# Constants of a hybrid encoder kernel packed so that the tiles TensorE reads begin at multiples of 512 bytes

## The chip, the core and the metric

The kernel runs on one core of a Trainium2 chip. The metric is the device time of one execution in microseconds (us); lower is better. Before the change the median of three runs is 2232.35 us (2230.22 to 2233.93).

The core's memory for operands, SBUF, has 128 partitions; a tile of shape 128 x 512 in float32 takes 2048 bytes in every partition. A tile's address is its byte offset within a partition. This text speaks of addresses by what is left of them after division by 512, and calls that the tile's **offset**.

## What is computed

The reference is a two-layer encoder on 512 tokens of width 1024, in float32. Cut to what matters here:

```python
for i in range(2):
    x = x + 0.5 * swiglu_ffn(rmsnorm(x, ffn1_norm[i]), ffn1_w1[i], ffn1_w2[i])
    h = rmsnorm(x, mix_norm[i])
    x = x + (s5_gla_mixer(h, ...) if i == 0 else retention_mixer(h, ...))
    x = x + 0.5 * swiglu_ffn(rmsnorm(x, ffn2_norm[i]), ffn2_w1[i], ffn2_w2[i])
return rmsnorm(x, final_norm)

def swiglu_ffn(h, w1, w2):              # w1: 1024 x 5632, w2: 2816 x 1024
    gate, up = jnp.split(h @ w1, 2, axis=-1)
    return (silu(gate) * up) @ w2
```

`s5_gla_mixer` holds a diagonal state-space model (S5) beside a gated linear attention, `retention_mixer` a retention layer; both are mostly projections by weight matrices as well.

## The kernel before, in words

**Arithmetic.** TensorE multiplies in `float32r`, which keeps fewer bits than float32. So each operand is split in two float32r tiles, a high part (`yh`, `wh`, `ph`, `qh`, `g`, `rh`, `vh`, `oh`, `ch`) and what is left (`yl`, `wl`, `pl`, `ql`, ...), and `mm3` (lines 193 to 195) makes three matmuls in place of one: high by high, high by low, low by high. In `T.matmul(ps, a, b)` the tile `a` is the *stationary* operand (a block of 128 x 128 that is loaded into the array first, the row LDWEIGHTS of the profile) and `b` the *moving* one (256 or 512 columns that stream through it). The profile names a matmul `mm<-b,a`: `mm<-y,wh` has `y` moving and `wh` stationary.

**Order of work.** The first FFN (`ffn`) uses plain products, with 512 moving columns. The three others (`ffn7`) cut each product of w1 into seven half-size products (Strassen's scheme): 256 moving columns, stationary blocks from `wh`/`wl` (raw weights, two of the seven), from `ph`/`pl` (sums of weights, four of the seven) and from `qh`/`ql` (one of the seven). Their second product by w2 again has 512 columns. The S5 part (line 843 and lines 885 to 887 among others) multiplies in full float32. Weights come by DMA from the SP queue, in order, into four buffers `raw` (line 177), ScalarE (ACT) and VectorE (DVE) split them, and for most of them a DMA from the GpSimd (POOL) queue adds `raw` into the low part (`lows`, line 189).

**Where tiles lie.** Pools are laid out one behind the other. The first pool, `const`, holds `x` (16384 bytes), then the small constants; behind it lie the pools `weights` (raw, wh, wl), `temps`, `operands` (the 28 tiles `y`), and behind these the pool of the stage that runs (`g`, `ph`, `pl`, `qh`, `ql`, `rh`, `vh`, ...). Almost every tile in these later pools is a multiple of 1024 bytes, so their offsets are all set by how many bytes the constants take, and by one small tile `rt` (128 x 2, two buffers of 32 bytes) in `temps`:

```python
gains = cp.tile([128, 7 * 8 + 4 + 16 + 4], F32, name="gains")          # 320 bytes
ident = cp.tile([128, 128], F32, name="ident")                         # 512
less = cp.tile([128, len(SEVEN) * 4], F32, name="less")                # 48, takes 64
rho8 = cp.tile([128, NG], F32, name="rho8")                            # 128
ones = cp.tile([128, 128], F32, name="ones")                           # 512
eps = cp.tile([128, 1], F32, name="eps")                               # 4, takes 32
```

`rho8` (decay rates of the S5 scan) is made early in the first FFN on ACT, and read by DVE in the mixer. `less` is used in `operand7`, `rt` in `finish`, the last norm at the end of the kernel.

Of the kernel before, what the change touches and what calls it, by code (L numbers as in the profile page):

```python
# [16 lines left out]
F32 = mybir.dt.float32  # L17
# [16 lines left out]
NG = 32  # L34
TWO_PI = 2.0 * math.pi
SEVEN = (2, 3, 5)
# [14 lines left out]
def encoder(tc, I, out, dbg=None):  # L51
    nc = tc.nc
    V, A, G, T = nc.vector, nc.scalar, nc.gpsimd, nc.tensor
    dma = nc.sync.dma_start
    f32 = lambda ap: ap.bitcast(F32)

    with ExitStack() as ctx:
        cp = ctx.enter_context(tc.tile_pool(name="const", bufs=1))
# [4 lines left out]
        dp = ctx.enter_context(tc.tile_pool(name="scratch", bufs=1, space=DRAM))  # L63
# [4 lines left out]
        yp = ctx.enter_context(tc.tile_pool(name="operands", bufs=28))  # L68
        ytile = lambda dt=F32R: yp.tile([128, S], dt, name="y", tag="y")
        yh, yl = [None] * KT, [None] * KT  # L70
        gains = cp.tile([128, 7 * 8 + 4 + 16 + 4], F32, name="gains")
        ident = cp.tile([128, 128], F32, name="ident")
        less = cp.tile([128, len(SEVEN) * 4], F32, name="less")
        minus = {(n, i): less[:, a * 4 + i:a * 4 + i + 1] for a, n in enumerate(SEVEN) for i in range(4)}
        rho8 = cp.tile([128, NG], F32, name="rho8")
        ones = cp.tile([128, 128], F32, name="ones")
        eps = cp.tile([128, 1], F32, name="eps")
        V.memset(ones, 1.0)
        V.memset(eps, EPS)
        norm_gain = lambda n, i: gains[:, n * 8 + i:n * 8 + i + 1]  # L80
# [7 lines left out]
        rd = dp.tile([4, 128, 2, 512], F32, name="rd")  # L88
        td = dp.tile([NG, 16, 15, 16], F32, name="td")
        ud = dp.tile([512, S], F32, name="ud")  # L90

        def tmp(tag, shape=(128, S), dt=F32):
            return tp.tile(list(shape), dt, name=tag, tag=tag)

        def bank(name="mm"):
            return pp.tile([128, S], F32, name=name, tag="mm")
# [173 lines left out]
        def ffn7(w1, w2, acc, nxt, gp, finish=None):  # L270
# [136 lines left out]
            for q, (ks0, ks1) in enumerate(CHUNKS):  # L407
# [85 lines left out]
                if finish is not None and not more:  # L493

                    steps = []
                    ws = [weights(w2q[n], True) for n in (KT - 2, KT - 1)]
                    for c in (left, right):
                        for n, w in zip((KT - 2, KT - 1), ws):
                            ps = bank()
                            for k in range(ks0, ks1):  # L500
                                second(n, ps, w, [k], ks1, c)
                                if steps and k % 2:
                                    next(steps[0], None)
                            residual(n, ps, c)
                            if n == KT - 2:
                                sq = tmp("tb", (128, H2))
                                A.activation(sq, x[n][:, c], AF.Square)
                                G.tensor_tensor(acc[:, c], acc[:, c], sq, op=ALU.add)
                        steps.append(finish(acc, c))
                    for _ in steps[1]:  # L510
                        pass
# [3 lines left out]
        def s5_prepare(wk):  # L515
# [25 lines left out]
            A.activation(cs, t1, AF.Sin)  # L541
            tt(t2, lr, dt, op=ALU.mult)
            A.activation(mag, t2, AF.Exp)
            A.activation(rho8, t2, AF.Exp, scale=float(TC))
            pr = wk.tile([128, TC + 1, NG], F32, name="pr")
            pi = wk.tile([128, TC + 1, NG], F32, name="pi")
            V.memset(pr[:, 0], 1.0)
# [169 lines left out]
            for st in range(NG // 4):  # L717
                finish(st, *built)
                if st < 7:
                    built = build(st + 1)  # L720
                if st == 2:
                    tabs = rotations()
                elif 3 <= st:
                    if st < 7:
                        rotate_table(st - 3, tabs)
                yield


        def s5_gla(acc, nxt, mp):
# [25 lines left out]
                to_chunks(j, project(W[j])[0])  # L755


            wgk = mp.tile([32, 512], F32, name="wgk")
            dma(wgk, I["wgk"])
            rmask = mp.tile([128, S], F32, name="rmask")  # L760
# [461 lines left out]
        with tc.tile_pool(name="g0a", bufs=14) as ga:  # L1222
            wk_pool = tc.tile_pool(name="s5work", bufs=1)
            wk = wk_pool.__enter__()
            wa = [wk.tile([128, 4, TC + 1, 16], F32, name=f"wa{i}") for i in range(2)]
            pieces = s5_prepare(wk)
            gb = []

            def filler(j):
                if j == 1:  # L1230
                    dma(ident, I["ident"])
                next(pieces, None)
                if j == 12:
                    for _ in pieces:
                        raise RuntimeError("S5 pieces left")
                    wk_pool.__exit__(None, None, None)
                    gb.append(ctx2.enter_context(tc.tile_pool(name="g0b", bufs=18)))

            with ExitStack() as ctx2:
                pick = lambda i: ytile() if i < 12 else (ga if i < 26 else gb[0]).tile([128, S], F32R, name="g", tag="g")  # L1240
                acc = ffn(I["ffn1_w1"][0], I["ffn1_w2"], acc, 1, pick, filler, first)
        show("ffn0")
        with tc.tile_pool(name="mix0", bufs=1) as mp:
            phase[0] = 1
            acc = s5_gla(acc, 2, mp)
            phase[0] = 0
# [14 lines left out]
        def finish(acc, c):  # L1261
            n, blocks = KT - 1, range(c.start // 128, c.stop // 128)
            last = tmp("tb", (128, S // 2))
            A.activation(last, x[n][:, c], AF.Square)
            st = sp.tile([128, S], F32, name="st", tag="st")
            rt = tmp("rt", (128, 2))
            yield
            for i, b in enumerate(blocks):
                T.matmul(st[:, i:i + 1], acc[:, b * 128:(b + 1) * 128], ones[:, 0:1], start=True, stop=False)
                T.matmul(st[:, i:i + 1], last[:, i * 128:(i + 1) * 128], ones[:, 0:1], start=False, stop=True)  # L1270
            A.activation(rt, st[:, 0:2], AF.Sqrt, bias=eps, scale=1.0 / D)
            V.reciprocal(rt, rt)
            diag = tmp("ta", (128, 256))
            for i in range(2):
                V.tensor_scalar_mul(diag[:, i * 128:(i + 1) * 128], ident, rt[:, i:i + 1])
            yield
            yield
            row = bank()
            T.matmul(row[:, 0:256], ones, diag, start=True, stop=True)
            if c.start == 0:  # L1280
                for i in range(n - 1):
                    A.activation(x[i], x[i], AF.Copy, scale=norm_gain(6, i))
            for i in (n - 1, n):
                A.activation(x[i][:, c], x[i][:, c], AF.Copy, scale=norm_gain(6, i))
            yield
            to = out.rearrange("(i p) t -> p i t", p=128)
            for t in (slice(0, 3), slice(3, 6), slice(6, 8)):
                V.tensor_tensor(xs[:, t, c], xs[:, t, c],
                                row[:, 0:256].unsqueeze(1).to_broadcast([128, t.stop - t.start, 256]), op=ALU.mult)
                dma(to[:, t, c], xs[:, t, c])  # L1290

        with tc.tile_pool(name="step3", bufs=1) as gp:
            ffn7(I["ffn2_w1"][1], w2(2), acc, None, gp, finish)
# [109 lines left out]
```

## Time and profile before

| | before |
|---|---|
| median of the runs | 2232.35 us |
| the profiled execution: its time / its span | 2233.29 us / 2231.5 us |
| granted TensorE clock, mean | 0.973 of 2.4 GHz |
| busy share of the span: PE, PEld | 95%, 83% |
| busy share of the span: DVE, ACT, POOL | 60%, 52%, 16% |
| matmuls | 12088 |

The span is the time from the first to the last instruction; the execution's own time has 1.8 us more around it. PE is TensorE's matmul side, PEld its weight loads. Matmuls are pipelined, so the busy time of one (its "mean ns") is longer than the step from one matmul's start to the next one's; the step is what a stream of matmuls costs, and it is read from a timeline as the difference of two starts over the number of matmuls between them.

### The profile page before, as it was taken

Reading aid. Unit: us, or ns where it says so; the run is one execution under the profiler, and the core shown is the slowest. Engines: PE = TensorE matmul, PEld = TensorE weight load, DVE = VectorE, ACT = ScalarE, POOL = GpSimd, SP = SyncE. Lnnn points to the kernel's source line nnn. Section 1 sums busy time; section 2 is a strip of 40 time slices with the busy share of each in tenths; the row PEclk is TensorE's granted clock in tenths of the full one; section 3 lists DMA queues with packets and bytes.
Section 4 is the critical chain, followed back from the end, with each engine's and each line's share of the span. In section 5 each row is a group of like instructions: output and inputs, shape, how many; then the busy total and the mean of one; then the engine's idle time right before and its main releaser. Section 6 shows DMA issues by size and latency. Waiting matters only on the chain.

```text
span 2231.5 us, 31247 instructions
## 1 busy us (share of the span) xinstructions
PE 2121.6 (95%) x12088; PEld 1844.2 (83%) x12088; DVE 1348.5 (60%) x2101; ACT 1169.2 (52%) x1696; POOL 363.8 (16%) x396
## 2 busy tenths in 40 slices
PE   8998999999998989999998999999999998999998
PEld 6877888777878889987988888778888887898897
DVE  7696210178748667568766566545444469766564
ACT  7444444462676454546655354455454557455453
POOL 3431112211021010103111010211111112010101
PEclk9999999998998999999999999999999999999999
DMA  8878888867565564554565464667676756564551
GB/s 233 212 196 220 196 191 189 229 171 210 133 151 143 151 148 139 144 145 123 141 158 154 125 145 120 165 163 176 152 180 151 172 138 159 141 156 137 148 155 48
DMA packets 125076, 357.50 MB, mean 160 GB/s; under 512 B 19808, under 2 KB 34528, under 8 KB 124800
## 3 DMA queue, kind: packets, MB, share of 16 engines
q0 software_dynamic: 41328, 133.19, 33.1%
q1 hardware_dynamic: 83600, 222.33, 29.7%
q8 instruction: 95, 1.56, 0.3%
q14 instruction: 53, 0.43, 0.1%
HBM read 208.17 MB, written 14.12 MB: 100 GB/s over the span
## 4 chain that ended last, share of the span: by engine, by line
PE 62%; DMA 12%; DVE 7%; issue 5%; ACT 5%; POOL 0%; SPq 0%; ACTq 0%; DVEq 0%; POOLq 0%
PE mm L193 20%; PE mm L194 20%; PE mm L195 20%; DMA raw<-in_ffn_w_dram 5%; DMA ql<-raw 4%; DMA wl<-raw 1%; ACT wl L188 1%; DVE pl L221 1%; ACT qh L324 1%; ACT ql L188 1%; ACT sv L336 0%; DMA raw<-in_w2a_dram 0%; DVE y L134 0%; PE st L1142 0%; DMA raw<-in_ab_in_dram 0%
## 5 line engine op out<-in xcount | busy, mean ns | idle before, releaser
L193 PE MATMUL mm<-y,wh 128*128 128x512 f32 (+1 forms) x1304 | 458.9, 352 | 7.9 <-ACT wh L1214 5.0
L195 PE MATMUL mm<-y,wl 128*128 128x512 f32 (+1 forms) x1304 | 454.9, 349 | 5.7 <-DMA wl<-raw 5.7
L194 PE MATMUL mm<-y,wh 128*128 128x512 f32 (+1 forms) x1304 | 456.1, 350 | 0.3 <-DVE y L103 0.3
L180 ACT CAST wh<-raw 128x1024 fp32r<-128x1024 f32 (+1 forms) x227 | 232.0, 1026 | 421.2 <-issue 190.4
L189 POOL DMA_DIRECT2D wl<-raw x221 | 190.7, 864 | 1290.1 <-ACT wl L188 1146.0
L193 PE MATMUL mm<-y,ph 128*128 128x256 f32 x1056 | 312.0, 296 | 59.2 <-ACT sv L336 41.0
L194 PE MATMUL mm<-y,ph 128*128 128x256 f32 x1056 | 308.6, 292 | 1.8 <-DVE y L134 1.8
L195 PE MATMUL mm<-y,pl 128*128 128x256 f32 x1056 | 307.9, 292 | 1.8 <-DVE pl L221 1.8
L193 PEld LDWEIGHTS mm<-y,wh 128*128 128x128 f32 x1304 | 249.2, 191 | 47.1 <-ACT wh L1214 5.4
L195 PEld LDWEIGHTS mm<-y,wl 128*128 128x128 f32 x1304 | 248.3, 190 | 41.0 <-DMA wl<-raw 7.7
L194 PEld LDWEIGHTS mm<-y,wh 128*128 128x128 f32 x1304 | 248.7, 191 | 35.0 <-DVE y L103 2.1
L193 PEld LDWEIGHTS mm<-y,ph 128*128 128x128 f32 x1056 | 211.7, 201 | 65.4 <-ACT sv L336 46.1
L193 PE MATMUL mm<-g,wh 128*128 128x512 f32 (+1 forms) x672 | 259.1, 387 | 0.6 <-ACT g L220 0.6
L194 PE MATMUL mm<-g,wh 128*128 128x512 f32 (+1 forms) x672 | 259.3, 387 | 0.0
L195 PE MATMUL mm<-g,wl 128*128 128x512 f32 (+1 forms) x672 | 258.8, 386 | 0.0
L188 ACT ACTIVATE wl<-raw 128x1024 fp32r<-128x1024 f32 x221 | 233.0, 1055 | 38.4 <-PE mm L194 23.4
L194 PEld LDWEIGHTS mm<-y,ph 128*128 128x128 f32 x1056 | 212.3, 201 | 2.7 <-DVE y L134 2.3
L195 PEld LDWEIGHTS mm<-y,pl 128*128 128x128 f32 x1056 | 211.9, 201 | 2.3 <-DVE pl L221 2.3
L221 DVE TENSOR_TENSOR pl<-sums,ph 128x1024 fp32r<-128x1024 f32 x132 | 160.7, 1222 | 77.2 <-ACT ph L220 76.7
L220 ACT CAST ph<-sums 128x1024 fp32r<-128x1024 f32 x132 | 137.4, 1050 | 68.1 <-PE mm L194 51.2
L193 PEld LDWEIGHTS mm<-g,wh 128*128 128x128 f32 x672 | 126.0, 188 | 27.1 <-ACT g L220 1.7
L195 PEld LDWEIGHTS mm<-g,wl 128*128 128x128 f32 x672 | 126.2, 188 | 26.1
(358 smaller groups left out, 3633.8 us busy)
## 6 DMA issues: line engine op xcount, KB each, us to landing
wl<-raw POOLq DMA_DIRECT2D x221, 512.0 KB, 5.5
raw<-in_ffn_w_dram SPq DMA_DIRECT2D x196, 512.0 KB, 4.0
raw<-in_w2b_dram SPq DMA_DIRECT2D x48, 512.0 KB, 3.3
raw<-in_ret_in_dram SPq DMA_DIRECT2D x48, 512.0 KB, 3.7
ql<-raw POOLq DMA_DIRECT2D x66, 256.0 KB, 4.5
raw<-in_w2a_dram SPq DMA_DIRECT2D x24, 384.0 KB, 3.7
raw<-in_ret_out_dram SPq DMA_DIRECT2D x16, 512.0 KB, 3.6
raw<-in_ab_in_dram SPq DMA_DIRECT2D x13, 512.0 KB, 4.9
```

What stands on the lines that cost most here:

```text
L180: A.copy(h[:, c], raw[:, c])
L188: A.activation(l, raw, AF.Copy, scale=-1.0)
L189: G.dma_start(l, raw, accum_op=ALU.add)
L193: T.matmul(ps, lh, rh, start=first, stop=False, skip_group_check=go_on)
L194: T.matmul(ps, lh, rl, start=False, stop=False, skip_group_check=go_on)
L195: T.matmul(ps, ll, rh, start=False, stop=last, skip_group_check=go_on)
L220: A.copy(hi, src)
L221: V.tensor_tensor(lo, src, f32(hi), op=ALU.subtract)
L324: A.copy(h, raws[j][1][:, hi4])
```

## The change

The small constants are put in one tile `columns` of 384 bytes (gains, less, eps as slices of it), and `rho8` no longer lives in `const`: ACT writes it to a tile of the S5 work pool, a DMA stores it in DRAM (`rhod`), and a second DMA loads it into a tile of the mixer's pool. `rt` becomes a slice of `less`.

```diff
-        gains = cp.tile([128, 7 * 8 + 4 + 16 + 4], F32, name="gains")
+        columns = cp.tile([128, 96], F32, name="columns")
+        gains, less, eps = columns[:, 0:80], columns[:, 80:92], columns[:, 92:93]
         ident = cp.tile([128, 128], F32, name="ident")
-        less = cp.tile([128, len(SEVEN) * 4], F32, name="less")
...
-        rho8 = cp.tile([128, NG], F32, name="rho8")
         ones = cp.tile([128, 128], F32, name="ones")
-        eps = cp.tile([128, 1], F32, name="eps")
...
+        rhod = dp.tile([128, NG], F32, name="rhod")
...
+            rho8 = wk.tile([128, NG], F32, name="rho8")
             A.activation(rho8, t2, AF.Exp, scale=float(TC))
+            dma(rhod, rho8)
...
+            rho8 = mp.tile([128, NG], F32, name="rho8")
+            dma(rho8, rhod)
             wgk = mp.tile([32, 512], F32, name="wgk")
...
-            rt = tmp("rt", (128, 2))
+            rt = less[:, c.start // 128:c.start // 128 + 2]
```

The offsets that the two built programs give their tiles:

| tiles | offset before | after |
|---|---|---|
| raw, wh, wl, and the temporaries (ta, tb, tc, rs, sumsq) | 160 | 0 |
| y, g, ph, pl, qh, ql, rh, rl, vh, vl, oh, ol, ch, cl, sums, sv | 224 | 0 |
| ident | 448 | 0 |
| ones | 128 | 0 |
| vm, wm, w1 of the S5 part | 96 | 0 |
| x (not read by TensorE) | 128 | 128 |

Blocks within these tiles begin at multiples of 512 bytes from the tile's start, so a block has its tile's offset. Before, 160, 224 and 96 are all 32 bytes past a multiple of 64.

The rows of PE, ACT, DVE and POOL stand in the same order in both programs, but for names and for two neighbours on ACT. The SP queue, which issues the loads, gets two more DMAs, and the load of `ident` moves ahead of one load of weights (the third of them, at the start of the kernel). The first place is early in the first FFN; `raw` are weights, `rho_350` is the program's name for the new tile `rho8`, and the brackets name the semaphores a row waits for. Before:

```order
L632 DMA dsk<-in_s5d_dram 16x64 [waits DMAHW3_49]
L177 DMA raw<-in_ffn_w_dram 128x1024 [waits DMAHW4_49,DMAHW5_49,DMASW0_49,Activation_49]
L177 DMA raw<-in_ffn_w_dram 128x1024 [waits DMAHW6_49,DMASW1_49,Activation_49]
L177 DMA raw<-in_ffn_w_dram 128x1024 [waits DMAHW7_49,DMASW2_49,Activation_49]
L177 DMA raw<-in_ffn_w_dram 128x1024 [waits DMAHW2_49,DMASW3_49,Activation_49]
```

And after:

```order
L634 DMA dsk<-in_s5d_dram 16x64 [waits DMAHW3_49]
L177 DMA raw<-in_ffn_w_dram 128x1024 [waits DMAHW4_49,DMAHW5_49,DMASW0_49,Activation_49]
L177 DMA raw<-in_ffn_w_dram 128x1024 [waits DMAHW6_49,DMASW1_49,Activation_49]
L546 DMA rhod<-rho_350 128x32 [waits Activation_49]
L177 DMA raw<-in_ffn_w_dram 128x1024 [waits DMAHW7_49,DMAHW0_49,DMASW2_49]
L177 DMA raw<-in_ffn_w_dram 128x1024 [waits DMAHW2_49,DMASW3_49,Activation_49]
```

The store of `rho8` stands between two loads of weights and waits for ACT. The second place is the start of the mixer's loads, near the end of the first FFN. After (before, the row L761 is missing, and nothing else differs but line numbers):

```order
L177 DMA raw<-in_ab_in_dram 128x1024 x6
L761 DMA rho_3471<-rhod 128x32
L763 DMA wgk<-in_wgk_dram 32x512
L767 DMA rmask<-in_rmask_dram 128x512
L768 DMA cmask<-in_cmask_dram 128x64
L771 DMA tb<-in_gmf_dram 128x512
L771 DMA tb<-in_gmb_dram 128x512
L177 DMA raw<-in_ab_in_dram 128x1024
```

The load of `rho8` is put ahead of the five loads of masks and gate weights.

## Rows read from the trace of the kernel before

**Rows 1.** The page, part 4: chain that ended last, shares of the span by engine.

```profile
PE 62%; DMA 12%; DVE 7%; issue 5%; ACT 5%; POOL 0%; SPq 0%; ACTq 0%; DVEq 0%; POOLq 0%
```

**Rows 2.** Groups by line and shape: count, busy us, mean ns, idle before.

```profile
L193 PE MATMUL mm<-y,ph 128*128 128x256 f32 x1056 | 312.0, 296 | 59.2 <-ACT sv L336 41.0 <-ACT ph L220 16.3 <-ACT y L132 1.9
L193 PE MATMUL mm<-y,wh 128*128 128x512 f32 x776 | 310.0, 400 | 7.9 <-ACT wh L1214 5.0 <-ACT y L102 2.4 <-ACT wh L180 0.3
...
L193 PE MATMUL mm<-g,wh 128*128 128x512 f32 x640 | 250.0, 392 | 0.6 <-ACT g L220 0.6
...
L193 PE MATMUL mm<-y,wh 128*128 128x256 f32 x528 | 148.9, 282 | 0.0
...
L193 PE MATMUL mm<-y,qh 128*128 128x256 f32 x264 | 74.8, 283 | 0.0
...
L193 PE MATMUL mm<-wh,y 128*128 128x512 f32 x160 | 63.8, 401 | 0.4 <-DVE tb L1070 0.4
...
L193 PE MATMUL mm<-oh,wh 128*128 128x512 f32 x128 | 49.7, 388 | 0.0
...
L193 PE MATMUL mm<-ph,vh 128*128 128x512 f32 x64 | 24.9, 393 | 0.0
```

**Rows 3.** Timeline of PE, 2002.9 to 2006 us: start, length, engine, line, instruction.

```profile
2002.62 0.28 PE L193 MATMUL mm<-y,qh 128*128 128x256 f32 x1
...
2004.06 0.28 PE L193 MATMUL mm<-y,wh 128*128 128x256 f32 x1
...
2005.42 0.28 PE L193 MATMUL mm<-y,ph 128*128 128x256 f32 x1
```

**Rows 4.** Timeline of PE, 1243 to 1248 us, first and last of 24.

```profile
1242.66 0.39 PE L194 MATMUL mm<-g,wh 128*128 128x512 f32 x1
...
1247.93 0.39 PE L193 MATMUL mm<-g,wh 128*128 128x512 f32 x1
```

**Rows 5.** Timeline of PE, 1478.4 to 1485 us, first and last of 24.

```profile
1478.45 0.39 PE L193 MATMUL mm<-ph,vh 128*128 128x512 f32 x1
...
1483.66 0.39 PE L195 MATMUL mm<-ph,vl 128*128 128x512 f32 x1
```

**Rows 6.** Timeline of PE, 1455 to 1460 us, first and last of 12.

```profile
1454.73 0.40 PE L194 MATMUL mm<-wl,y 128*128 128x512 f32 x1
...
1457.30 0.39 PE L193 MATMUL mm<-wh,y 128*128 128x512 f32 x1
```

**Rows 7.** Timeline of PE, 425.1 to 428.4 us, first and last of 8.

```profile
425.37 0.63 PE L193 MATMUL mm<-y,wh 128*128 128x512 f32 x1
...
428.36 0.44 PE L194 MATMUL mm<-y,wh 128*128 128x512 f32 x1
```

**Rows 8.** Windows: busy by engine, granted clock (0.50), DMA share, GB/s.

```profile
425.10:428.40 3.30, 3.30 (x10) 2.53 (x9) 0.00 (x0) 0.00 (x0) 0.00 (x0) 0.50 0.99 199
```

**Rows 9.** Timeline of PE in the S5 part, float32 matmuls (two records each).

```profile
544.74 3.40 PE L843 MATMUL mm<-U,vm 128*128 128x64 f32 x29
...
551.40 0.38 PE L885 MATMUL mm<-w,U 128*64 128x128 f32 x2
...
553.14 0.38 PE L887 MATMUL mm<-wm,xi 128*64 128x128 f32 x2
```

**Rows 10.** Timelines of SP, ACT and DVE at the places of rho8.

```profile
30.62 5.49 SPq L177 DMA_DIRECT2D raw<-in_ffn_w_dram  x2
...
30.90 0.21 ACT L544 ACTIVATE rho<-small 128x32 f32<-128x32 f32 x1
...
423.92 1.03 SPq L759 DMA_DIRECT2D wgk<-in_wgk_dram  x1
...
499.43 0.68 DVE L833 TENSOR_TENSOR tc<-rho,cmask 128x512 f32<-128x512 f32 x1
```

**Rows 11.** Groups by line and shape: two DVE instructions.

```profile
L390 DVE TENSOR_TENSOR x<-x,ta 128x512 f32<-128x512 f32 x70 | 47.5, 687 | 1.1
...
L379 DVE TENSOR_TENSOR ta<-ta,rs 128x512 f32<-128x512 f32 x66 | 45.4, 687 | 0.8
```

## The prediction, made before the changed kernel was run

> **What bounds the kernel now.** First I read the chain of work that ended last, because only what lies on it can shorten the span: TensorE (PE) holds 62% of the 2231.5 us, DMA 12%, DVE 7%, ACT 5% [rows 1]. So the step from one matmul to the next is the largest price in this kernel. Second I read how many matmuls of each kind there are [rows 2]. Each row there is one of three lines (193 to 195) of equal count, so a count is taken three times: 4632 matmuls with 512 columns whose stationary block is in `wh`/`wl` (3 x (776 + 640 + 128)), 480 with the weights moving and `y` stationary (3 x 160), 192 with `vh`/`vl` (3 x 64); 3960 with 256 columns and `ph` or `qh` stationary (3 x (1056 + 264)), 1584 with 256 columns and `wh` (3 x 528).
>
> Third I read the step of each kind from timelines, in stretches without a wait, and set the offsets of both operands beside it:
>
> - 256 columns, `y` (offset 224) with `qh` (224): 12 matmuls in 1.44 us, 120.0 ns each; directly behind them the same `y` with `wh` (160): 12 in 1.36 us, 113.3 ns [rows 3].
> - 512 columns, `g` (224) with `wh` (160): 23 in 5.27 us, 229 ns [rows 4].
> - 512 columns, `ph` (224) with `vh` (224): 23 in 5.21 us, 226.5 ns [rows 5].
> - 512 columns, `wh` (160) moving with `y` (224): 11 in 2.57 us, 233.6 ns [rows 6].
>
> At 2.4 GHz one column per clock would be 106.7 and 213.3 ns. Times 2.4, the five steps are 288, 272, about 550, 544 and 560 clocks: 16 to 48 clocks too many. Two things stand in these rows. The surplus depends on where the operands lie: in rows 3 the moving tile, the shape, the neighbours and the engines are the same, and only the stationary tile changes, from offset 224 to 160, and with it 6.7 ns. And it is a matter of supply, not of the array: where the granted clock is 0.50 (1.2 GHz) [rows 8] the same 512 columns take 427 ns (7 in 2.99 us) [rows 7], which is 512 clocks of 1.2 GHz with no surplus. Full float32, which spends two clocks on a column, shows hardly any either: 128 columns take 108.8 ns (16 records in 1.74 us from L885 to L887), 256 clocks and 5 more [rows 9], though all its tiles too lie 32 bytes past a multiple of 64.
>
> **The change, part by part.** PE's program stays as it is, row for row; what moves is every operand, from 224 or 160 to 0.
>
> *Matmuls.* No matmul before has both operands at a multiple of 64 bytes, so the new step has no row and is bounded from both sides. My reading of the surplus: 16 float32r columns are 64 bytes, and a stream that begins 32 bytes past a multiple of 64 touches one piece of 64 bytes more than it holds: 17 for 16 (272 clocks), 33 for 32 (528). What then remains of the rows with equal offsets (288, 544) is 16 clocks in both, a collision of the two streams. After the change all operands have equal offsets and no extra piece: 288 - 16 = 272 clocks, 113.3 ns, for 256 columns, and 544 - 16 = 528, 220.0 ns, for 512. In sum:
>
> - 4632 x (229 - 220.0) = 41.7 us
> - 192 x (226.5 - 220.0) = 1.2 us
> - 480 x (233.6 - 220.0) = 6.5 us
> - 3960 x (120.0 - 113.3) = 26.5 us
> - 1584 x (113.3 - 113.3) = 0
>
> Together 75.9 us. (Some 400 matmuls of smaller groups, `ch`, `rh` and the last halves of `g`, are left out; they would add about 2 us.) The best end for this price is a step with only float32's 5 clocks more than its columns: 517, 215.4 ns, for 512. For 256 columns the loading of the stationary block sets a floor: the row of L843, where 64 columns hardly hide it, has 28 steps in 3.40 - 0.27 = 3.13 us, 111.8 ns for a block of 128 [rows 9]. These give 4632 x 13.6 + 192 x 11.1 + 480 x 18.2 + 3960 x 8.2 + 1584 x 1.5 = 63.0 + 2.1 + 8.7 + 32.5 + 2.4 = 108.7 us. The worst end is the dearest row of each length: 233.6 and 120.0 ns, 33.3 us more than now (4632 x 4.6 + 192 x 7.1 + 1584 x 6.7). I take the middle price, since it is the only one that explains 272, 288 and 544 by whole pieces; about 550 and 560 need one collision more, which I can't derive.
>
> *How much of it reaches the end.* The mean clock is 0.973, so 5.4% of the span is at 1.2 GHz, where nothing is gained: at most 0.946 x 75.9 = 71.8 us. As lower bound I take PE's part of the chain alone: the matmuls counted above fill 4632 x 0.229 + 192 x 0.2265 + 480 x 0.2336 + 3960 x 0.12 + 1584 x 0.1133 = 1871 us, 75.9 is 4.1% of that, and 4.1% of 62% of the span is 56 us; the rest would be given back as longer waits for DMA, ACT and DVE. The middle is 64 us, 84% of the sum.
>
> *The store of rho8* stands on SP between two loads of weights. ACT makes it from 30.90 to 31.11 us; SP issued a load at 30.62 and the next at about 35.8 (the row holds two issues and ends at 36.11) [rows 10]. So the store falls in a free interval of some 4 us: nothing. If ACT were 5 us later there, loads of weights would wait behind it.
>
> *The load of rho8* stands ahead of `wgk` at 423.92 us, whose issue took 1.03 us [rows 10], so what is behind it on SP is up to 1 us late; DVE reads rho8 at 499.43 us, 75 us later. 0 to 1 us; I take 0, because the load of weights behind the masks fills a buffer ahead of its use. The load of `ident`, ahead of the third load of weights, is 64 KB and also nothing.
>
> *Other engines.* `x` already lies at a multiple of 64 before, the temporaries do not; a DVE instruction that writes `x` and one that stays in temporaries have the same 687 ns [rows 11]. So DVE and, by the same measure, ACT gain nothing.
>
> *DMA.* No row tells two offsets of one transfer apart. On the chain DMA has 12% [rows 1], 268 us. I take 0. The Trainium skill, "DMA: Bandwidth & Descriptors", section "How a descriptor splits into AXI transactions", says that a descriptor that does not start on a multiple of 256 bytes pays for the bytes before it; by that, a row of `raw` (4096 bytes at offset 160) would fall from 133 beats of 32 bytes to 128, an estimated 3.8%, or up to 10 us of the chain's DMA. No run here shows it yet.
>
> The sum against the profiled execution's 2233.3 us (0.9 us above the median): 2233.3 - 64 = 2169 us.
>
> **The rivals.**
>
> *The full price goes* (the best end above): 0.84 x 108.7 = 92 us, 2142 us; if no wait gives any back, 0.946 x 108.7 = 103 us, 2130. For it speaks that float32 shows 5 clocks at any offset; against it that equal offsets still cost 288 where 160 against 224 cost 272, so a collision is there that alignment need not remove.
>
> *Only the relation of the two operands counts.* Then all pairs get the price of the equal pairs, 120.0 and 226.5 ns: -4632 x 2.5 - 480 x 7.1 + 1584 x 6.7 = -4.4 us, 2229.6 us. For it speaks that each kind's step is fixed by a pair of offsets; against it nothing in the rows, since the equal pair at 224 is also 32 past a multiple of 64.
>
> *Nothing changes.* The steps would be set by something that goes along with the tile and not with its offset, such as its place in memory. Then 2233 us. Against it: `y` and `oh`, far apart, show the same kind of step with `wh`. The Trainium skill, "SBUF — State Buffer", section "Specifications (TRN2)", speaks for this rival: it gives SBUF lines of 16 bytes, and every tile before begins at a multiple of 32 already, so by it there is nothing to straddle. Rows 3 differ from that page, in that 64 bytes of offset change the step.
>
> *Slower: both streams begin at the same place.* With all offsets 0, the moving and the stationary stream start on the same piece every time, and the collision grows to that of the dearest rows. If only the 256-column matmuls with `wh` go to 120.0 ns, it is 1584 x 6.7 = 10.6 us, 2243 us; at the worst end 0.946 x 33.3 = 31.5 us, 2265 us. It decides as soon as the 512-column step is above 229 ns. For it: the equal pair is the dearer one at 256 columns. Against it: at 512 it is the cheapest.
>
> **How the numbers follow.** The middle price 0.43, the full price 0.17, the relation alone 0.13, nothing 0.09, slower 0.18. About 0.2%, 4.5 us, is what a measurement here can tell from no change. Faster by more than that: the first two and a small part of the third, 0.62; the rest of the third and the fourth, 0.20; slower 0.18. The point is that of the likeliest, 2169 us; its own range is 2155 to 2185. The range for 8 in 10 has to take in the full price and the cases near no change: 2125 to 2245; about 0.05 lies below (a gain of DMA on top), 0.12 above.
>
> **What would show it.** Timelines of PE after: 256-column steps at 113.3 ns for `ph` and `qh` as for `wh`, and 512-column ones at 220.0 ns in all three kinds; at 1.2 GHz still 427 ns. 120.0 and 226.5 would show the relation alone, 111.8 and 215.4 the full price. Beside it idle time of PE that ends on DMA or ACT should grow by some 8 to 20 us. The prediction is wrong if the steps stay or grow, or if they shrink as said and the span doesn't, since the chain then goes over to the loads.

## The result and the profile after

The change made the kernel faster by half a per cent, a fifth of what was forecast: 2219.02 us (median of 12 runs, 2212.49 to 2229.49) against 2231.24 us (12 runs), ratio 0.9948 with a 95% interval of 0.9933 to 0.9963, so about 12 us and not 64. Three further comparisons of the same two kernels gave 0.9935, 0.9953 and 0.9951. The profiled execution below is the slowest of the 12 (2229.49 us, span 2227.7), so steps are read from it and no gain.

The chain that ended last, of the changed kernel, answers to [rows 1]: PE's share fell by 3 points and "issue", time in which nothing that the profile shows was waited for, rose by 3. It says less than it seems to: in three further executions of the same kernel PE holds 59%, 50% and 62%, so shares of one chain don't carry an effect of 0.5%.

```profile
PE 59%; DMA 13%; issue 8%; DVE 7%; ACT 5%; POOL 1%; SPq 0%; ACTq 0%; DVEq 0%; POOLq 0%
```

Timelines of PE in the changed kernel (start, length, engine, line, instruction), in the order of [rows 3], [rows 4], [rows 5] and [rows 6]; last, at the lower clock, [rows 7], with its window as [rows 8].

```profile
1998.09 0.28 PE L193 MATMUL mm<-y,qh 128*128 128x256 f32 x1
...
1999.53 0.28 PE L193 MATMUL mm<-y,wh 128*128 128x256 f32 x1
...
2000.97 0.28 PE L193 MATMUL mm<-y,ph 128*128 128x256 f32 x1
```

```profile
1243.73 0.39 PE L194 MATMUL mm<-g,wh 128*128 128x512 f32 x1
...
1247.36 0.39 PE L195 MATMUL mm<-g,wl 128*128 128x512 f32 x1
```

```profile
1476.69 0.39 PE L193 MATMUL mm<-ph,vh 128*128 128x512 f32 x1
...
1481.91 0.39 PE L195 MATMUL mm<-ph,vl 128*128 128x512 f32 x1
```

```profile
1443.70 0.39 PE L193 MATMUL mm<-wh,y 128*128 128x512 f32 x1
...
1449.14 0.39 PE L193 MATMUL mm<-wh,y 128*128 128x512 f32 x1
```

```profile
441.96 0.63 PE L193 MATMUL mm<-y,wh 128*128 128x512 f32 x1
...
445.38 0.63 PE L195 MATMUL mm<-y,wl 128*128 128x512 f32 x1
```

```profile
441.90:445.80 3.90, 3.90 (x10) 2.97 (x9) 0.00 (x0) 0.00 (x0) 0.00 (x0) 0.50 1.05 281
```

Both 256-column streams of 12 matmuls now take 1.44 us, 120.0 ns a step: `wh` lost the 6.7 ns that it had over `qh`. All 512-column steps are alike: 16 in 3.63 us (226.9), 23 in 5.22 (227.0), 24 in 5.44 (226.7). At granted clock 0.50 it is 427 ns (8 in 3.42 us), as before. These are the steps of the rival "only the relation of the two operands counts", 120.0 and 226.5, in every kind.

Groups of the changed kernel by line and shape (count, busy us, mean ns, idle before): PE's wait for ACT's copies to `sv` is 39.2 us, in [rows 2] 41.0.

```profile
L193 PE MATMUL mm<-y,ph 128*128 128x256 f32 x1056 | 309.8, 294 | 57.6 <-ACT sv L336 39.2 <-ACT ph L220 16.4 <-ACT y L132 1.9
L193 PE MATMUL mm<-y,wh 128*128 128x256 f32 x528 | 152.4, 289 | 0.0
```

### The profile page after: what moved, and what is told of

The parts are those of the page before. It is cut to its first block, busy times and chain, and to the rows that moved or that the text cites. A ratio compares the mean times of both kernels' runs of the same rounds, so it can differ in the third digit from the quotient of the medians.

```text
span 2227.7 us, 31250 instructions
## 1 busy us (share of the span) xinstructions
PE 2115.4 (95%) x12088; PEld 1851.1 (83%) x12088; DVE 1348.3 (61%) x2101; ACT 1169.9 (53%) x1696; POOL 363.4 (16%) x396
## 4 chain that ended last, share of the span: by engine, by line
PE 59%; DMA 13%; issue 8%; DVE 7%; ACT 5%; POOL 1%; SPq 0%; ACTq 0%; DVEq 0%; POOLq 0%
PE mm L193 19%; PE mm L194 19%; PE mm L195 19%; DMA raw<-in_ffn_w_dram 6%; DMA ql<-raw 4%; DMA wl<-raw 2%; ACT wl L188 1%; ACT qh L324 1%; ACT ql L188 1%; DVE pl L221 1%; POOL wl L189 0%; ACT sv L336 0%; DVE y L134 0%; PE st L1146 0%; DVE wl L182 0%
## 5 line engine op out<-in xcount | busy, mean ns | idle before, releaser
L193 PE MATMUL mm<-y,ph 128*128 128x256 f32 x1056 | 309.8, 294 | 57.6 <-ACT sv L336 39.2
L193 PEld LDWEIGHTS mm<-y,wh 128*128 128x128 f32 x1304 | 251.8, 193 | 44.8 <-ACT wh L1218 5.0
L194 PEld LDWEIGHTS mm<-y,wh 128*128 128x128 f32 x1304 | 252.3, 193 | 33.5 <-issue 1.4
L297 ACT CAST wh<-raw 128x1024 fp32r<-128x1024 f32 x66 | 69.3, 1050 | 149.3 <-DMA raw<-in_ffn_w_dram 99.1
```

The costliest lines, as they stand in the source:

```text
L193: T.matmul(ps, lh, rh, start=first, stop=False, skip_group_check=go_on)
L194: T.matmul(ps, lh, rl, start=False, stop=False, skip_group_check=go_on)
L297: A.copy(h, up)
```

## The experiments

Three theories about the step of a matmul stood against each other. **Pieces** (the prediction's): each stream that begins 32 bytes past a multiple of 64 pays. **Relation**: only the difference of the two operands' offsets counts. **The tile**: something that goes with the tile and not with its offset. What else made the 12 us, the DMAs' offsets or the moved constants, was asked beside it. Each experiment is the changed kernel with pads, tiles that nothing uses, unless said otherwise. "Before" is timed anew on the chip of each group.

**1. Offsets by themselves.** This kernel computes no encoder, only streams of matmuls and DMAs:

```diff
+for cols in (512, 256):
+    for r in range(0, 512, 32):
+        group(f"d{r}at0c{cols}x", cols, r, 0)
...
+            T.matmul(ps[:, 0:cols], sta[:, s:s + 128], mov[:, m:m + cols], start=n == 0, stop=n == count - 1)
...
+            G.dma_start(cut(lows[at], at), cut(raws[at], at), accum_op=ALU.add)
```

> This kernel leaves out the whole encoder: it runs 25 float32r matmuls in a row for each pair of offsets (stationary r bytes past the moving one, r from 0 to 480 in steps of 32, and a few pairs at other absolute offsets), with 512 and with 256 columns, and then six loads and six adding DMAs of 512 KB for each of seven offsets. Theory 'relation': the step depends on the difference of the two offsets alone; difference 0 gives 226.7 ns at 512 and 120.0 at 256 at any absolute offset (0, 32, 224), difference -64 gives about 229 and 113.3, +64 about 233 at 512. Rival 'pieces of 64 bytes' (the prediction's): a pair at absolute offset 0 or 64 is some 6.7 ns cheaper than the same difference at 32 or 224. For the adding DMAs, theory 'the DMA's own offset': packets of 4096 bytes at 32, 160 and 224 take about 3% longer (338 against 328 ns in the kernels) than at 0, 128 and 256; rival: no difference by offset, the kernels' 10 ns come from what ran beside them.

Timeline of PE in this kernel; `d192at0` means that the stationary block lies 192 bytes past the moving one, which lies at 0, and `dm64` that it lies 64 below.

```profile
62.66 5.84 PE L72 MATMUL d0at0c512x<-mov,sta 128*128 128x512 f32 x25
68.33 5.99 PE L72 MATMUL d32at0c512x<-mov,sta 128*128 128x512 f32 x25
74.16 6.00 PE L72 MATMUL d64at0c512x<-mov,sta 128*128 128x512 f32 x25
80.00 6.00 PE L72 MATMUL d96at0c512x<-mov,sta 128*128 128x512 f32 x25
...
97.48 5.90 PE L72 MATMUL d192at0c512x<-mov,sta 128*128 128x512 f32 x25
103.22 5.99 PE L72 MATMUL d224at0c512x<-mov,sta 128*128 128x512 f32 x25
109.05 5.84 PE L72 MATMUL d256at0c512x<-mov,sta 128*128 128x512 f32 x25
114.72 5.99 PE L72 MATMUL d288at0c512x<-mov,sta 128*128 128x512 f32 x25
...
155.44 5.83 PE L72 MATMUL d0at32c512x<-mov,sta 128*128 128x512 f32 x25
161.11 5.85 PE L72 MATMUL d0at224c512x<-mov,sta 128*128 128x512 f32 x25
166.79 6.00 PE L72 MATMUL d64at32c512x<-mov,sta 128*128 128x512 f32 x25
172.63 6.00 PE L72 MATMUL d64at64c512x<-mov,sta 128*128 128x512 f32 x25
178.47 5.98 PE L72 MATMUL d64at224c512x<-mov,sta 128*128 128x512 f32 x25
184.29 5.89 PE L72 MATMUL dm64at224c512x<-mov,sta 128*128 128x512 f32 x25
190.01 5.84 PE L72 MATMUL d16at0c512x<-mov,sta 128*128 128x512 f32 x25
195.69 6.00 PE L72 MATMUL d48at0c512x<-mov,sta 128*128 128x512 f32 x25
```

From start to start over 25: difference 0 gives 5.67 us, 226.8 ns, at offsets 0, 32 (5.67) and 224 (5.68) alike; 64 gives 5.84, 233.6, at 0, at 32 and at 64, and 5.82 at 224; 192 gives 5.74, 229.6, and -64 gives 5.72, 228.8; and 256 is like 0 (5.67). Where a stream of 512 columns begins costs nothing; the difference decides, counted modulo 256. "Pieces" falls here, and "the tile" too, since the same two tiles are read in every row.

With 256 columns the picture is less clean. Difference 0 takes 118.8 to 120.4 ns at 0, 32 and 224, and -64 takes 113.6, as the theory says. But a difference of 64 takes 118.0 ns at offset 0 and 117.6 at 64, and 114.4 at 32 and 114.0 at 224. That is not the absolute offset, because a difference of 320 at offset 0, the same modulo 256, takes 114.4 as well. Group 4 comes back to it.

**2. Relation and absolute offset crossed in the whole kernel.** `undo` restores the old offsets (160 and 224) and keeps the rest of the change, `eq224` puts all operands at 224, `rel64` makes the old difference of 64 out of multiples of 64 (weights at 0, `y` and stages at 64).

```diff
+        cp.tile([128, 40], F32, name="pad")                        # undo; eq224: 56 columns; rel64: none
...
+                tp.tile([128, 16], F32, name="padt", tag="padt", bufs=1)   # undo and rel64
```

> The changed kernel with two unused pads, so that raw, wh, wl lie at 160 and y and the stage tiles at 224 again, as before; the store and load of rho8 and the slices stay. If the offsets do everything: 2231 us as before (2227 to 2235), steps 113.3 and 228.9 ns for wh, 233.3 for the moving weights, 120.0 for ph and qh, adding packets 338 ns. If the constants' new places or the moved rho8 do a part of the 12 us: below 2227.

> The changed kernel with one unused pad, so that all operands lie at the same offset 224, 32 past a multiple of 64. Theory 'relation' for the matmuls: steps of the changed kernel, 120.0 and 226.7 ns in every kind. Rival 'pieces of 64 bytes': other steps than in the changed kernel. If in addition the DMAs pay for their own offset, adding packets take 338 ns and the time is about 8 us above the changed kernel, near 2227 us; if they do not, 2219 us.

> The changed kernel with one unused pad of 64 bytes ahead of y: weights at 0, y and the stage tiles at 64, so the relation of before (stationary wh 64 below the moving y) at multiples of 64. Theory 'relation': the steps of before, 113.3 and 228.9 ns for wh, 233.3 for moving weights, 120.0 for ph and qh, which is 4 us more than in the changed kernel. With the DMAs' own offset as second cause (raw and wl at 0): packets 328 ns and about 2223 us; if the relation did all of the 12 us, 2231 us.

Before 2231.48 us; `undo` 2229.80, ratio 0.9996 (0.9981 to 1.0011); `rel64` 2230.42, 0.9995 (0.9981 to 1.0009); `eq224` 2224.89, 0.9970 (0.9954 to 0.9986). Timelines of PE, first `eq224`, then `rel64`:

```profile
1990.24 0.28 PE L194 MATMUL mm<-y,qh 128*128 128x256 f32 x1
...
1991.68 0.28 PE L194 MATMUL mm<-y,wh 128*128 128x256 f32 x1
...
1993.12 0.28 PE L194 MATMUL mm<-y,ph 128*128 128x256 f32 x1
```

```profile
1997.56 0.28 PE L193 MATMUL mm<-y,qh 128*128 128x256 f32 x1
...
1999.00 0.28 PE L193 MATMUL mm<-y,wh 128*128 128x256 f32 x1
...
2000.36 0.28 PE L193 MATMUL mm<-y,ph 128*128 128x256 f32 x1
```

`eq224`, no operand at a multiple of 64, has the new steps (1.44 and 1.44 us for 12); `rel64`, every operand at one, has the old ones (1.44 and 1.36). So has the time: the two kernels with the old difference are as slow as before, the one with equal offsets is faster, at 2224.89 us between its two forecasts (2219 and 2227). `undo` also shows that the rest of the change, the store and load of `rho8` and the packed constants, has no effect that these runs can tell (-0.2% to +0.1%).

**3. A worse and two supposedly better relations.** `up64` puts the stationary `wh` 64 above the moving operand, all at multiples of 64. `ph192` leaves everything equal but `ph`, `pl`, `qh`, `ql`, which go 64 below. `y64` puts `y` 64 above `wh`, `ph` and `qh`, with the other stage tiles equal to `wh`. The changed kernel ran beside them.

```diff
+        cp.tile([128, 16], F32, name="pad")                                # up64
...
+                tp.tile([128, 48], F32, name="padt", tag="padt", bufs=1)   # up64; y64: 16 columns
...
+                yp.tile([128, 48], F32, name="pady", tag="pady", bufs=1)   # y64
...
+                gp.tile([128, 48], F32, name="padp", tag="padp", bufs=1)   # ph192, ahead of ph
...
+                gp.tile([128, 16], F32, name="padg", tag="padg", bufs=1)   # ph192, behind ql
```

> The changed kernel once more, beside the three below, for a second profiled execution and a tighter median: 2219 us (2215 to 2223) by every theory.

> The changed kernel with two unused pads: the weights at 64, y and the stage tiles at a multiple of 256, so the stationary wh lies 64 bytes above the moving operand; every offset is still a multiple of 64. Theory 'relation': 512 columns with wh stationary rise from 226.7 to 233.3 ns, some 4820 matmuls by 6.7 ns, 32 us; those with y stationary go to 229 ns, 1 us; 256 columns with wh fall to 114 to 118 ns, at most 11 us back. The first product of the first FFN (1268 matmuls, 298 us whatever the offsets so far) waits for loads and can hide 8 us of the 32. In sum 2219 + 13 to 33: 2232 to 2252 us, slower than before. Rival 'alignment of each stream' (what counts is that all begin at multiples of 64): 2219 us.

> The changed kernel with two unused pads: weights at 0, y at 64, the stage tiles at a multiple of 256, so ph, qh and wh all lie 64 below the moving y with 256 columns, and wh equal to g, oh and ch with 512. Theory 'relation': 113.3 ns for all 5640 matmuls with 256 columns, 6.7 ns each, 37.6 us; 229 ns with wh and y at 512 (some 2400, +5.5 us), 233.3 with the moving weights (480, +3.2 us); 226.7 for g, oh, ch. Sum 29 us, of which the waits for ACT in the w1 part of the seven products may take half: 2190 to 2205 us. If PE's step is not what bounds those parts: 2219 to 2228 us.

> The changed kernel with two unused pads around ph, pl, sv, qh, ql alone, which puts these 64 bytes below a multiple of 256; all else stays equal. Theory 'relation': 256 columns with ph and qh 113.3 ns (3960 by 6.7 ns, 26.4 us), all else as in the changed kernel. If half reaches the end: 2206 us (2193 to 2215); if the w1 part of the seven products waits for ACT and not for PE's step, 2219 us.

Before 2234.26 us; the changed kernel 2218.97, 0.9935 (0.9912 to 0.9957); `up64` 2248.90, 1.0068 (1.0051 to 1.0084); `y64` 2224.68, 0.9966 (0.9947 to 0.9984); `ph192` 2214.14, 0.9914 (0.9896 to 0.9932). Timeline of PE in `up64`, then in `ph192`, and the group of `ph192` that waits for `sv`:

```profile
1253.29 0.39 PE L194 MATMUL mm<-g,wh 128*128 128x512 f32 x1
...
1258.89 0.39 PE L194 MATMUL mm<-g,wh 128*128 128x512 f32 x1
```

```profile
1994.22 0.28 PE L193 MATMUL mm<-y,qh 128*128 128x256 f32 x1
...
1995.58 0.28 PE L193 MATMUL mm<-y,wh 128*128 128x256 f32 x1
...
1997.02 0.28 PE L193 MATMUL mm<-y,ph 128*128 128x256 f32 x1
```

```profile
L193 PE MATMUL mm<-y,ph 128*128 128x256 f32 x1056 | 303.0, 287 | 64.7 <-ACT sv L338 46.5 <-ACT ph L220 16.4 <-ACT y L132 1.9
```

`up64`: 24 steps in 5.60 us, 233.3 ns, and 30 us above the changed kernel beside it, inside its forecast: neat offsets with a bad difference are the slowest kernel of all. `ph192`: `qh` now at 113.3 ns (1.36 us) and `wh` at 120.0, the mirror image of [rows 3]; but of the 26 us forecast in steps only 5 us arrive (2214 us, at the upper edge of its 2193 to 2215), and PE's wait for `sv` grows from 36.1 to 39.2 us in the changed kernel's four profiled executions to 46.5 us. `y64` missed its forecast (2190 to 2205) by far. It lies in the range that was to hold if PE's step were not the bound (2219 to 2228), but the steps themselves did not come: its 256-column streams run at neither 113.3 nor 120.0 ns.

```profile
1994.99 0.28 PE L193 MATMUL mm<-y,qh 128*128 128x256 f32 x1
...
1996.40 0.28 PE L193 MATMUL mm<-y,wh 128*128 128x256 f32 x1
...
1997.82 0.28 PE L193 MATMUL mm<-y,ph 128*128 128x256 f32 x1
```

12 take 1.41 to 1.42 us there, 117.7 ns. Why, the next group asks; so it does what is left of the DMAs.

**4. Absolute offsets again, and how a stream begins.** `eq64` and `eq32` put all operands at 64 or 32 (one pad of 16 or 8 columns, as in `eq224`). `m2_entry` is again no encoder: 256-column streams behind different neighbours, then adding DMAs beside still and busy engines.

```diff
+    group("equal", 256, 0)
+    group("less64_behind_equal", 256, 448)
+    group("wide", 512, 0, 0, 24)
+    group("less64_behind_wide", 256, 448)
```

> The changed kernel on the chip of the three others, as their yardstick: 2219 us (2216 to 2223). At a mean granted clock of 0.977 it should stand at 2222, since runs of one kernel fall by 1.2 to 1.6 us for each 0.001 of clock.

> The changed kernel with one unused pad of 64 bytes, all operands at offset 64: the same relation, a multiple of 64 and not of 256. Steps 120.0 and 226.7 ns by every theory. If the adding DMAs pay only for 32 bytes past a multiple of 64: packets 328 ns, time as the changed kernel on this chip within 2 us. If they pay for every offset that is no multiple of 256 (the rule of the Trainium skill's page on descriptors): packets 338 ns, 3 to 6 us above it.

> The changed kernel with one unused pad of 32 bytes, all operands at offset 32: the same relation. Steps 120.0 and 226.7 ns. If the adding DMAs' 338 ns packets reach the end: 3 to 6 us above the changed kernel on this chip. If they don't, and the equal pair at 224 was 6 us slower by its clock and by chance: within 2 us of it.

> This kernel leaves out the whole encoder. First part: 48 matmuls with 256 columns in a row, stationary 64 bytes below the moving operand, behind different neighbours. Theory 'two steady states': behind a stream of equal offsets at 256 columns the step is 113.3 ns, behind 512 columns or a pause of PE it is 117.7 ns and stays so to the end of the stream. Rival: the step is one of the two by the pair alone, whatever came before. Second part: six adding DMAs of 512 KB at offsets 0, 64, 32 and 160, first with VectorE and ScalarE still, then with VectorE busy, then with ScalarE busy. Theory 'contention': packets take 327 ns at all offsets when the engines are still, and at 32 and 160 up to 10 ns more beside busy engines, but not at 0 and 64. Rival: 327 ns in all twelve, so that something else in the encoder made 338 ns.

Before 2235.04 us; the changed kernel 2223.56, 0.9953 (0.9936 to 0.9970); `eq64` 2225.41, 0.9955 (0.9939 to 0.9971); `eq32` 2226.64, 0.9967 (0.9952 to 0.9982): by their intervals the three can't be told apart (`eq64` stands 1.9 us above the changed kernel, `eq32` 3.1). Timeline of PE in `m2_entry`, twice the same order:

```profile
66.05 5.60 PE L73 MATMUL less_behind_equal<-mov,sta 128*128 128x256 f32 x48
71.49 5.63 PE L73 MATMUL wide<-mov,sta 128*128 128x512 f32 x24
76.96 5.81 PE L73 MATMUL less_behind_wide<-mov,sta 128*128 128x256 f32 x48
82.61 5.91 PE L73 MATMUL equal_b<-mov,sta 128*128 128x256 f32 x48
...
147.34 5.60 PE L73 MATMUL less_behind_equal<-mov,sta 128*128 128x256 f32 x48
152.78 5.63 PE L73 MATMUL wide<-mov,sta 128*128 128x512 f32 x24
158.25 5.81 PE L73 MATMUL less_behind_wide<-mov,sta 128*128 128x256 f32 x48
163.90 5.91 PE L73 MATMUL equal_b<-mov,sta 128*128 128x256 f32 x48
```

The same pair runs at 5.44 / 48 = 113.3 ns behind a stream of equal offsets and at 5.65 / 48 = 117.7 ns behind 512 columns, both times, to the end of the stream. A stream 64 below has two steady states, and here the neighbour ahead goes with which. (The streams behind a pause began at the lower granted clock and tell nothing.) A stream 64 above has the same two steps, but not by the same rule: behind a stream 64 below it takes 113.3 ns the first time and 117.7 the second, behind equal offsets 117.7 both times. In `y64` no 256-column stream has equal offsets, so hardly any is ever brought into the better state.

On DMAs: median packet times of the adding DMAs (4096 bytes) are 338 ns before, 338 in `undo`, 339 in `eq224`, 334 in `eq32`, 335 in `eq64`, and 328 in the changed kernel and in `rel64`. So in the encoder they do go with the DMA's own offset, and 64 is not enough. The Trainium skill, "DMA: Bandwidth & Descriptors", section "How a descriptor splits into AXI transactions", says that a descriptor that does not start on a multiple of 256 bytes pays for the bytes before it. In direction the encoder's adding packets agree with that: off such a multiple they take 1.8 to 3.4% longer, and at 160, where the prediction's estimate was 3.8%, 3.0%. The loads into `raw`, rows of the same 4096 bytes, show nothing of it: plain load packets of that size take 159 ns in the median in every one of these kernels. Nor do the adding DMAs without the encoder: 327 to 328 ns at all seven offsets in `m1_offsets`, and in `m2_entry` medians of 331 to 336 ns at 0, 64 and 32 and 339 to 340 at 160, the last of the four to run, engines still or busy alike. "Contention with busy engines" falls by that, and so does its rival (327 ns in all twelve); what makes a packet longer stays open. No effect on the time can be told: `rel64`, with 328 ns, is no faster than `undo`, and `eq64`, with 335, and `eq32`, with 334, lie within the intervals of the changed kernel.

**5. What is open of the cause.** `ph192` and the changed kernel on one chip, and `y64q`, which is `y64` with `qh` and `ql` equal to `y`. The mixers' tiles (`oh`, `ch` and others) lie at 64 there too, 64 above `wh`, where `y64` had them equal to it.

```diff
+            for tag in ("qh", "ql"):
+                for _ in range(2):
+                    gp.tile([128, 512], F32R, name="early", tag=tag, bufs=2)
+            gp.tile([128, 48], F32, name="padq", tag="padq", bufs=1)
```

> The changed kernel as yardstick on the chip of the two others: 2219 to 2224 us.

> The kernel with ph and qh 64 bytes below y once more. If about 40% of the 26.4 us of steps reach the end: 11 us below the changed kernel on this chip. If a fifth: 5 us. If nothing does: the same time. PE's idle time that ends on ACT's copies to sv should again be 6 to 8 us above the changed kernel's 38 to 39 us.

> The changed kernel with y at 64, wh, ph and pl at multiples of 256, and qh, ql equal to y. Theory 'two steady states': after each stream of qh (120.0 ns) the streams of wh and ph that follow run at 113.3 ns instead of the 117.7 ns of y64, until 512 columns come between; most of the 4752 matmuls with wh and ph. Rival 'the pair alone' (the 117.7 belongs to y at 64 with wh at 0): 117.7 ns throughout. In time both 2212 to 2224 us, since 512 columns with y or oh and wh cost 229 ns here.

Before 2231.33 us; the changed kernel 2221.13, 0.9951 (0.9934 to 0.9967); `ph192` 2216.22, 0.9925 (0.9896 to 0.9953), again 5 us less, with 45.9 us of waiting for `sv`; `y64q` 2225.28, 0.9969 (0.9951 to 0.9987), a little above its range. Timeline of PE in `y64q`:

```profile
1990.74 0.28 PE L193 MATMUL mm<-y,wh 128*128 128x256 f32 x1
...
1992.15 0.28 PE L193 MATMUL mm<-y,qh 128*128 128x256 f32 x1
...
1993.58 0.28 PE L193 MATMUL mm<-y,wh 128*128 128x256 f32 x1
...
1994.94 0.28 PE L193 MATMUL mm<-y,ph 128*128 128x256 f32 x1
```

`wh` takes 1.41 us for its 12 ahead of `qh` and 1.36 behind it. Over the whole trace, 49 of 57 streams directly behind one of `qh` run at 113.3 ns, 17 of 18 behind 512 columns and 30 of 32 behind an idle PE at 117.7. The states are there in the encoder too, and the rival (the pair alone) falls. What enters which state is only partly known: the 512 columns ahead in `m2_entry`, and nearly all in `y64q`, have equal offsets. Where they are 64 below themselves, 2 of 9 streams of `y` with `wh` behind them run at 113.3 ns in `before`, 4 of 9 in `undo` and 7 of 9 in `rel64`, and the others at 117.7.

**Where the time went, by stage.** The lengths below are differences between the starts of each stage's first matmul, worked out from the profiled executions, one for each run; single ones scatter by some us (the parts with 256 columns take 786 to 792 us with the old difference, 792 to 797 in the changed kernel and 790 to 802 in `eq224`, `eq64` and `eq32`).

| us | old difference (before, `undo`, `rel64`) | changed kernel (4 executions) | `up64` | `ph192` (2) |
|---|---|---|---|---|
| first FFN, up to its product by w2 | 297.8 | 297.0 | 301.8 | 299.6 |
| first FFN, product by w2 | 116.7 | 115.6 | 119.0 | 115.6 |
| mixer | 248.0 | 246.3 | 247.8 | 244.3 |
| `ffn7`, parts with 256 columns | 790.2 | 793.9 | 787.6 | 781.8 |
| `ffn7`, products by w2 | 340.2 | 337.9 | 345.3 | 338.7 |
| retention | 432.4 | 426.8 | 435.7 | 426.4 |

`eq224`, `eq64` and `eq32` have the changed kernel's lengths where 512 columns stream: 337 to 338 us in the products by w2 and 426 to 428 in retention. So the relation shows at the very stages where its steps changed.

## Why the prediction was right and wrong

*The direction* was right, and the time lies in the range, but in part by luck: 26.5 of the 75.9 us of steps were to come from 256 columns with `ph` and `qh`, whose step did not change, and `wh` there got dearer. The forecast gain was five times too large.

*The step that failed* is the price of the alignment, under "Matmuls": 17 pieces for 16, so 113.3 ns for all 256 and 220.0 for all 512 columns. No absolute offset has such a price (`eq224`, `eq32`, `eq64`, and 0 against 32 and 224 in `m1_offsets`). In its place the 512 columns with `wh` went from 229 to 226.9 ns, the 256 columns with `ph` and `qh` stayed at 120.0, and those with `wh` rose from 113.3 to 120.0. The five steps of [rows 3 to 6] are the difference alone: `wh` 64 below `y` or `g`, `y` 64 above `wh`, or equal. I fitted a model of pieces to 272, 288 and 544 clocks and put it at 0.43, while the rival that needed no model, with nothing against it in the rows, had 0.13. The rows even held a test: of two pairs that both lie 32 past a multiple of 64, the prediction had to add a "collision" that it could not derive. Why the difference of two addresses matters inside the chip, no run here shows.

*The rival's sum* was -4.4 us; measured are -12. So its steps came true and its time did not. With the steps measured, counted in full, it is 4632 x 2.3 + 480 x 6.7 - 1584 x 6.7 = 3.3 us of gain. By stage, the 512-column parts gain about what their steps say, 1.1 + 2.3 + 5.6 = 9.0 us (counts times the change of step give an estimated 1.0, 2.6 and 4.9; the parts ahead of the first w2 product, 0.8, and the mixer, 1.7, are within their scatter). The 256-column parts, where `wh` got dearer by 10.6 us (9 by the mean steps of the traces, as some streams of before had 117.7 ns), lose only 3.7, with a scatter of the same size; PE's waits for `sv` fell there from 42.2 us, the mean of the three kernels with the old difference, to 37.5. The missed term is thus how unequally a step reaches the end: fully in products by w2 and in retention, and by these differences for about a third to a half in the parts with 256 columns, where PE also waits for `sv`. `ph192` shows the same from the other side: 26 us of steps forecast, 12 us in that stage (793.9 to 781.8, part of its streams in the dearer state), some 9 us more waiting for `sv` (46.5 and 45.9), 5 us in time. The prediction's 84% for all kinds was therefore wrong as well. The idle time of PE that was to grow by 8 to 20 us did not grow either: the span less PE's busy time is 105 to 112 us in the changed kernel and 110 to 111 with the old difference.

*What is left.* The stages sum to -7.8 us, the comparisons give -10 to -15. Part of that goes with the mean granted clock: over the 24 runs of before beside `undo` the time falls by 1.2 us for each 0.001 of it, and in the three comparisons with both clocks on record the changed kernel's is 0.0015 to 0.0034 higher, so 2 to 4 us; why it is higher is not shown. Equal offsets alone gain 0.30 to 0.45% (`eq224`, `eq32`, `eq64`), which is most of the change's 0.47 to 0.65%. Whether the DMAs' offsets add 2 or 3 us or nothing, these runs can't tell: the kernels with equal offsets and longer packets stand at 0.9955, 0.9967 and 0.9970, the changed kernel at 0.9935 to 0.9953, but `rel64`, with the short packets, gains nothing on `undo`.

*Costed at nothing and confirmed within that bound*: the moved `rho8` and the packed constants (`undo`). *No step at 1.2 GHz changes*: confirmed (427 ns). *The float32 row* was read by the record: a float32 matmul of 128 columns has two records there and takes 217.5 ns, so about four clocks of 2.4 GHz for a column, and the 215.4 ns built on its 5 clocks were reached in no run. *The rival "same place"* had the one thing right that `wh` goes to 120.0 ns when offsets are equal; its 512 columns did not grow, and the parts with 256 columns hid most of its 10.6 us.

## What to carry to other kernels

When a matmul's step depends on addresses, compare the two operands with each other before comparing either with a boundary, and test it by a kernel that moves both together. What a dearer or cheaper step is worth differs by stage: here the same nanosecond counted about fully where PE ran without a wait and by roughly a third to a half where it also waited for ACT's copies. Of the kernels tried, the fastest is `ph192`: equal offsets where 512 columns stream, and 64 below where 256 do; at 0.9914 and 0.9925 it beats the kernel before clearly, and the changed one by 5 us twice, with intervals that overlap.

## What the runs showed that was not expected

The period of the relation is 256 bytes: differences of 0 and 256 give 226.8 ns at 512 columns, 192 and -64 229.6 and 228.8, the others tried 232 to 234, but for 16 bytes with 227.2. And 256-column streams whose stationary block lies 64 below have two steady steps, 113.3 and 117.7 ns: behind 256 columns of equal offsets mostly the first, behind 512 columns of equal offsets or an idle PE mostly the second.
